# Expert blocks and query weights loaded in pairs, with one more block ahead of the parked ones

## The chip, the cores and the metric

The kernel runs on one core of a Trainium2 chip. The metric is the device time of one execution in microseconds (us). Three runs of the kernel before took 2314.72, 2319.04 and 2312.84 us, median 2314.72. Engines are called PE (matmul), DVE (vector), ACT (scalar), POOL (GpSimd) and SP (sync, which here only issues DMAs).

## What is computed

Two transformer blocks over 512 tokens of width 1024, in fp32. The first block ends in a product-key expert layer, and this is where the change lies. Cut to what matters:

```python
def peer(xn, w_query, sub_keys, u_tab, v_tab):          # per chunk of 128 tokens
    q = (xc @ w_query).reshape(c, PEER_HEADS, 2, D_HALF)
    sc = jnp.einsum('chpd,hpkd->chpk', q, sub_keys)      # 8 heads, 2 halves, 128 keys
    sv, si = lax.top_k(sc, PEER_TOPK)                    # 16 of 128, twice
    ...                                                  # 16 of the 256 pairs: idx, g
    a = gelu(jnp.einsum('chkd,cd->chk', u_tab[idx], xc))
    return jnp.einsum('chk,chkd->cd', g * a, v_tab[idx]) # u_tab, v_tab: 16384 x 1024
```

Every token uses 8 x 16 = 128 of the 16384 experts. The second block (`dilated_mixture_attention`, `spatial_gating` and a gated feed-forward) is not touched.

## The kernel before, in words

All large products are done as three matmuls on fp32r parts (`mm3`, lines 135 to 138): a weight block is loaded raw, ACT copies it to the part `whi` and DVE subtracts to get `wlo`. `wload` (lines 125 to 133) does so for one block of 128x1024 fp32, 4096 bytes per partition, from a pool with three raw buffers and, in the expert stage, four buffers each of `whi` and `wlo` (pool `wpb`, line 399).

The expert layer is done in two ways. Token tile 0 gathers its 2 x 128 expert rows per token by indirect DMA from POOL (`gather_steps`, lines 458 to 477). Tiles 1 to 3 (384 tokens) meet all 16384 experts in 128 dense blocks of 128 experts: the first product (`hps`, 24 matmuls of 384 columns), Gelu, a multiplication with the gate matrix, and the second product into six accumulators (`acc`, 18 matmuls of 512 columns). Three stages follow each other:

1. Routing (about 380 to 880 us). Sixteen blocks of query weights (line 509), the top-16 searches on DVE, then `gate_matrix`, which writes the dense gate matrix to DRAM as `wdr`. Between these steps `park_blocks` computes the first product of 68 expert blocks (`NPARK`, blocks `NLEAD` to `NLEAD` + 67) and stores it in DRAM as `park`. The instruction order of this stage is the planner's, which works from its own costs.
2. The lead (about 880 to 908 us), lines 706 to 717: the `NLEAD` = 3 blocks in front of the parked ones are split and multiplied.
3. The dense loop (908 to 1699 us), lines 719 to 734: iteration n loads what block n+3 needs (`dload`), splits v of block n+2 and u of block n+2 where it is not parked (`dsplit`), does `h_stage(n+1)` and then the second product `v_stage(n)`. For a parked block `h_stage` only reloads `hg` from `park`. Every eighth iteration begins with `wtile`, which reads the next eight blocks' slab of the gate matrix, 1536 KB in runs of 512 bytes, into one of two `wt` buffers; the slab before last must have been used up by `hw` (line 685).

Lead and loop stand in `tc.manual_schedule()`: there each engine issues its instructions in the order in which the code emits them, and an instruction that waits holds up all behind it on its engine. In the loop v blocks use the pool `wd`, with three raw and three split buffers of 4096 bytes per partition.

Of the kernel before, what the change touches and what calls it, by code (L numbers as in the profile page):

```python
# [8 lines left out]
F32 = mybir.dt.float32  # L9
F32R = mybir.dt.float32r  # L10
# [3 lines left out]
AF = mybir.ActivationFunctionType  # L14
# [8 lines left out]
NEG = -1e30  # L23
NPARK = 68                                # blocks of expert activations computed during the routing
NLEAD = 3                                 # blocks in front of the parked ones
PARKS = ((), (2, 1), (2, 2), (2, 1))      # parked blocks per group of a tile's gate matrix, even and odd
GATH = (0, 1, 3, 3)                       # gathers per group of a tile's gate matrix
RATE = (0.9, 2.5)                         # gathers per dense block, parked and not
DECODE = {(1, 1): 0, (1, 4): 2, (2, 3): 3}
# [12 lines left out]
def body(ctx: ExitStack, tc: tile.TileContext, A: dict, out: bass.AP):  # L42
# [13 lines left out]
    def sqrt_ahead(after):  # L56
        """Has the activation table of Sqrt loaded before the chain that needs it."""
        w = sm.tile([128, 1], F32, name="warm", bufs=1)
        SC.activation(w, after, AF.Square)
        SC.activation(w, w, AF.Sqrt)  # L60
# [13 lines left out]
    def rstd_newton(var, which):  # L74
        """1 / sqrt(var + eps) by three Newton steps from the exponent-halving guess, on the vector engine alone."""
        w = sm.tile([128, 4], F32, name="nw")
        x, y, a, r = [w[:, k:k + 1] for k in range(4)]
        V.tensor_scalar(x, var, (1e-5, 1e-6)[which], None, op0=OP.add)
        V.tensor_scalar(a.bitcast(U32), x.bitcast(U32), 1, None, op0=OP.logical_shift_right)
        V.tensor_scalar(y.bitcast(U32), a.bitcast(U32), -1.0, 1597463007.0, op0=OP.mult, op1=OP.add)  # L80
        for c in (-3.0, -12.0, -768.0):
            V.scalar_tensor_tensor(a, x, y, y, op0=OP.mult, op1=OP.mult)
            V.scalar_tensor_tensor(y, a, c, y, op0=OP.add, op1=OP.mult)
        V.tensor_scalar(r, y, -1.0 / 8192.0, None, op0=OP.mult)
        return r
# [14 lines left out]
    def first_half(junk_pool, y):  # L100
        """mean square of a row's first half, halved, plus the norm's eps"""
        ss = sumsq(junk_pool, y, 512)
        b = sm.tile([128, 1], F32, name="half")
        V.tensor_scalar(b, ss, 1.0 / D, 1e-6, op0=OP.mult, op1=OP.add)
        return b
# [48 lines left out]

    def halves(mm_pool, srcs, xh, xl, fill, parts=(0, 1)):
        """The blocks of srcs, two token tiles ahead of the other two; fill() readies those."""
        ws = [wload(src, [128, ND, 128]) for src in srcs]
        pss = [mm_pool.tile([128, S], F32, name="mm", tag="mm") for _ in srcs]
        for part in parts:
            sl = slice(part * 256, part * 256 + 256)  # L160
            if part == parts[1]:
                fill()
            for (wh, wl), ps in zip(ws, pss):
                fm_block(ps[:, sl], wh, wl, xh[:, :, sl], xl[:, :, sl], ND)
        return pss
# [25 lines left out]

    # ------------------------------------------------ first block: mixers
    with ExitStack() as st:
# [14 lines left out]
        with ExitStack() as s1:  # L208
            wk = s1.enter_context(tc.tile_pool(name="wkn", bufs=2, reuse_waits="tile"))
            xts = []  # L210
            for t in range(NT):
                xt = wk.tile([128, D], F32, name="xt", bufs=4)
                SY.dma_start(xt, A["x"][t * 128:(t + 1) * 128, :])
                xts.append(xt)
                if t == 0:
                    g_mix = gain("g_mix")
                    SY.dma_start(ident, A["ident"])

            def xs_of(t):
                xt = xts[t]  # L220
                r = rstd_of(sumsq(wk, xt, D), D, 0)
                xs = wk.tile([128, D], F32, name="xs")
                V.scalar_tensor_tensor(xs, xt, r, g_mix, op0=OP.mult, op1=OP.mult)
                return xs

            to_feature(pst, xs_of, xh, xl, (0, 1))
            first[8], first[9] = halves(pmm, [A["w_in"][8], A["w_in"][9]], xh, xl,
                                        lambda: to_feature(pst, xs_of, xh, xl, (2, 3)))
# [166 lines left out]

    # ------------------------------------------------ product-key experts
    # token tile 0 gathers its expert rows; the other tiles meet every expert on the tensor engine
    with ExitStack() as st:
        wp = st.enter_context(tc.tile_pool(name="wpb", bufs=4, reuse_waits="tile"))
        wps.append(wp)  # L400
# [24 lines left out]
        with ExitStack() as s1:  # L425
            wk = s1.enter_context(tc.tile_pool(name="wk2", bufs=2, reuse_waits="tile"))
            pst = s1.enter_context(tc.tile_pool(name="pst2", bufs=2, space=PSUM, side="right", reuse_waits="tile"))

            def xs_of(t):
                xt = hres[:, t, :]  # L430
                r = rstd_of(sumsq(wk, xt, D), D, 0)
                xs = xtok if t == 0 else wk.tile([128, D], F32, name="xs")
                V.scalar_tensor_tensor(xs, xt, r, gff, op0=OP.mult, op1=OP.mult)
                return xs

            with tc.high_priority():
                to_feature(pst, xs_of, xh, xl, (0, 1))

            def rest():
                with tc.high_priority():  # L440
                    to_feature(pst, xs_of, xh, xl, (2, 3))

            first = halves(pmm, [A["w_query"][0], A["w_query"][1]], xh, xl, rest)

        def h_block(n):
            uh, ul = wload(A["u_cols"][n], [128, ND, 128])
            ps = psh.tile([128, TD], F32, name="hps", tag="hps")
# [5 lines left out]
        def park_blocks():  # L453
            for n in range(NPARK):
                SY.dma_start(park[n], h_block(NLEAD + n))
                yield

# [28 lines left out]
        with mix as s1:  # L486
# [18 lines left out]
            for hp_ in range(16):  # L505
                if hp_ < len(first):
                    ps = first[hp_]
                else:
                    wh, wl = wload(A["w_query"][hp_], [128, ND, 128])
                    ps = pmm.tile([128, S], F32, name="mm", tag="mm")  # L510
# [14 lines left out]
                if hp_ % 2 == 0:  # L525
                    continue
                # a pair (a, b) has (a + 1)(b + 1) - 1 pairs before it in the order, so b < 4 once a >= 4
                h = hp_ // 2
# [111 lines left out]
        def dload(kind, n):  # L640
            if n >= 128:
                return
            if kind == "u":
                if parked(n):
# [3 lines left out]
                    return  # L648
                pool, src = wp, A["u_cols"][n].rearrange("p k j -> p (k j)")
            else:  # L650
                pool, src = wd, A["v_experts"][n * 128:(n + 1) * 128, :]
            raw = pool.tile([128, D], F32, name="wraw", tag="wraw", bufs=3)
            SY.dma_start(raw, src)
            raws[kind, n] = raw

# [49 lines left out]
        with tc.manual_schedule():  # L705
# [3 lines left out]
            for m in range(3):  # L709
                dload("v", m)  # L710
            dload("u", NLEAD)
            for m in range(NLEAD):
                dsplit("u", m)
            for m in range(2):
                dsplit("v", m)
            for m in range(NLEAD):
                h_stage(m)
            done = 0
            for n in range(128):
                if n % 8 == 0:  # L720
                    wtile(n // 8 + 1)
                dload("v", n + 3)
                if n + 3 > NLEAD:
                    dload("u", n + 3)
                if n + 2 >= NLEAD:
                    dsplit("u", n + 2)
                dsplit("v", n + 2)
                want = int(min(n + 1, 71) * RATE[0] + max(n - 70, 0) * RATE[1])
                spread(gathers, (want - done) // 2)
# [17 lines left out]

    # ------------------------------------------------ second block
    with ExitStack() as st:
# [9 lines left out]
        with ExitStack() as s2:  # L759
# [193 lines left out]
            def to_y(c, t, ps):  # L953
# [3 lines left out]
                else:  # L957
# [7 lines left out]
                    if t > 1:  # L965
# [3 lines left out]

            pss = halves(pmm, [A[w][c] for c in range(2) for w in ("w_gate", "w_up")], x4h, x4l,  # L970
                         lambda: to_feature(pst, lambda t: yt[:, t, :], x4h, x4l, (1, 0)), (1, 0))
# [55 lines left out]


def _part(v):
    return np.ascontiguousarray(v.reshape(-1, 128).T)  # L1030


def prepare(I):
# [17 lines left out]
    A["w_o"] = _rows(I["w_o"][0])  # L1051
    A["w_query"] = _cols(I["w_query"][0])
    A["sub_keys"] = I["sub_keys"][0].reshape(16, 128, 128).transpose(0, 2, 1)
    A["u_experts"] = I["u_experts"][0]
    A["u_cols"] = I["u_experts"][0].reshape(128, 128, ND, 128).transpose(0, 3, 2, 1)
    A["v_experts"] = I["v_experts"][0]
    A["ln_final_g"] = I["ln_final_g"]
    A["positions"] = _part(I["positions_2"][0])
# [38 lines left out]
```

## Time and profile before

| | us |
|---|---|
| median of three runs | 2314.72 |
| lowest and highest | 2312.84, 2319.04 |
| span of the profiled execution | 2313.5 |
| expert stage within it | about 380 to 1699 |

The profiled execution's span is 1.2 us below the median of the runs; nothing else of it lies outside the span in what is shown. The page lists for each engine its busy time, in 40 slices of the span how busy it was, which clock PE was granted, and how busy the 16 DMA engines were. For a change in one stage the questions are which engine is busy without a gap there, and what the gaps wait for.

### The profile page before, as it was taken

To read this page: it belongs to the slowest core of one execution; us is meant where nothing else is said; L and a number is where in the kernel's file an instruction comes from. 1 tells how busy PE (TensorE), PEld (TensorE's weight loads), DVE (VectorE), ACT (ScalarE), POOL (GpSimd) and SP (SyncE) were. 2 spreads that over 40 slices of the span, in tenths; PEclk is the share of its full clock that TensorE was granted. 3 is DMA by queue.
4 is the path that set the end of the run, shared out by engine and by line. 5 is a ranking of instruction groups with operands and counts; after the bars stand their busy time and mean duration, and the time that the engine had idled before them with its cause. 6 is when DMAs were issued, how large, how long until landed. Compare 5 with 4: busy or idle time off the path is not lost.

```text
span 2313.5 us, 30184 instructions
## 1 busy us (share of the span) xinstructions
PE 2246.8 (97%) x11337; PEld 1931.4 (83%) x11337; DVE 1495.2 (65%) x2998; ACT 986.1 (43%) x1631; POOL 382.4 (17%) x261
## 2 busy tenths in 40 slices
PE   7999998999899999999999999999999999999998
PEld 6768887989799999777779999999976778888886
DVE  4553254989999994767777777777784555333323
ACT  4354233333897783333333333333353364322222
POOL 0000000000222430323323444444400000000000
PEclk9999999999899999999999999999999999999999
DMA  5202232443577997889899898889732112333331
GB/s 173 92 19 75 90 111 84 128 125 118 213 272 289 363 350 253 295 311 329 293 323 322 306 320 297 296 302 323 274 113 74 56 55 87 105 101 93 98 100 65
DMA packets 177572, 444.82 MB, mean 192 GB/s; under 512 B 15249, under 2 KB 84241, under 8 KB 174353
## 3 DMA queue, kind: packets, MB, share of 16 engines
q1 hardware_dynamic: 140560, 308.65, 39.8%
q0 software_dynamic: 36864, 134.23, 16.3%
q8 instruction: 89, 1.46, 0.2%
q14 instruction: 59, 0.48, 0.1%
HBM read 402.19 MB, written 40.63 MB: 191 GB/s over the span
## 4 chain that ended last, share of the span: by engine, by line
PE 86%; DVE 5%; ACT 4%; DMA 4%; issue 1%; DVEq 0%; ACTq 0%; SPq 0%
PE mm L136 13%; PE mm L137 12%; PE mm L138 12%; PE hps L138 7%; PE hps L136 7%; PE hps L137 7%; PE acc L136 6%; PE acc L138 6%; PE acc L137 6%; DMA wraw<-in_v_experts_dram 3%; PE wps L612 2%; PE sc L311 1%; PE pv L346 1%; ACT stg L614 1%; PE sc L889 1%
## 5 line engine op out<-in xcount | busy, mean ns | idle before, releaser
L130 ACT ACTIVATE whi<-wraw 128x1024 fp32r<-128x1024 f32 x232 | 241.8, 1045 | 568.9 <-PE mm L137 343.0
L132 DVE TENSOR_TENSOR wlo<-wraw,whi 128x1024 fp32r<-128x1024 f32 x232 | 278.7, 1204 | 265.9 <-ACT whi L130 261.5
L136 PE MATMUL hps<-x2h,whi 128*128 128x384 f32 x1024 | 348.1, 340 | 2.1 <-ACT whi L130 1.8
L138 PE MATMUL hps<-x2h,wlo 128*128 128x384 f32 x1024 | 345.1, 337 | 0.8 <-DVE wlo L132 0.8
L137 PE MATMUL hps<-x2l,whi 128*128 128x384 f32 x1024 | 344.2, 336 | 0.0
L464 POOL DMA_INDIRECT gu<-in_u_experts_dram,ix x128 | 190.8, 1491 | 914.0 <-PE wps L612 605.5
L136 PE MATMUL acc<-whi,hh 128*128 128x512 f32 x768 | 302.6, 394 | 17.3 <-ACT hh L117 17.3
L138 PE MATMUL acc<-whi,hl 128*128 128x512 f32 x768 | 303.2, 395 | 0.0
L137 PE MATMUL acc<-wlo,hh 128*128 128x512 f32 x768 | 302.7, 394 | 0.0
L664 DVE TENSOR_TENSOR wlo<-wraw,whi 128x1024 fp32r<-128x1024 f32 x188 | 227.5, 1223 | 74.6 <-ACT whi L662 69.0
L662 ACT ACTIVATE whi<-wraw 128x1024 fp32r<-128x1024 f32 x188 | 198.3, 1056 | 171.3 <-issue 85.5
L473 POOL DMA_INDIRECT gv<-in_v_experts_dram,ix x128 | 189.7, 1482 | 380.7 <-DVE hres L475 275.3
L136 PEld LDWEIGHTS hps<-x2h,whi 128*128 128x128 f32 x1024 | 193.3, 189 | 5.4 <-ACT whi L130 2.1
L137 PEld LDWEIGHTS hps<-x2l,whi 128*128 128x128 f32 x1024 | 193.1, 189 | 2.7
L138 PEld LDWEIGHTS hps<-x2h,wlo 128*128 128x128 f32 x1024 | 193.1, 189 | 1.1 <-DVE wlo L132 1.1
L136 PEld LDWEIGHTS acc<-whi,hh 128*128 128x128 f32 x768 | 145.5, 189 | 49.6 <-ACT hh L117 21.0
L138 PEld LDWEIGHTS acc<-whi,hl 128*128 128x128 f32 x768 | 145.8, 190 | 33.3 <-DVE hl L118 2.7
L137 PEld LDWEIGHTS acc<-wlo,hh 128*128 128x128 f32 x768 | 145.7, 190 | 29.3
L475 DVE SCALAR_TENSOR_TENSOR hres<-gv,ga,hres 128x1024 f32<-128x1024 f32 x128 | 164.1, 1282 | 1.0
L466 DVE CUSTOM_DVE_ANT_0 gu<-gu,xtok 128x1024 f32<-128x1024 f32 x128 | 154.5, 1222 | 0.0
L137 PE MATMUL mm<-x4l,whi 128*128 128x512 f32 (+1 forms) x384 | 143.9, 375 | 0.0
L136 PE MATMUL mm<-x4h,whi 128*128 128x512 f32 (+1 forms) x384 | 143.3, 376 | 0.3 <-ACT x4h L117 0.3
(316 smaller groups left out, 4022.3 us busy)
## 6 DMA issues: line engine op xcount, KB each, us to landing
wraw<-in_u_cols_dram SPq DMA_DIRECT2D x128, 512.0 KB
wraw<-in_v_experts_dram SPq DMA_DIRECT2D x128, 512.0 KB
wraw<-in_w_in_dram SPq DMA_DIRECT2D x50, 512.0 KB
wdr<-stg SPq DMA_DIRECT2D x24, 1024.0 KB
wt<-wdr SPq DMA_DIRECT2D x16, 1536.0 KB
park<-hg SPq DMA_DIRECT2D x68, 192.0 KB
hg<-park SPq DMA_DIRECT2D x68, 192.0 KB
wraw<-in_w_gate_dram SPq DMA_DIRECT2D x22, 512.0 KB
```

Source lines behind the costliest of these rows:

```text
L130: SC.activation(hi, raw, AF.Copy)
L132: V.tensor_tensor(lo, raw, f(hi), op=OP.subtract)
L136: PE.matmul(ps, lhsT=ah, rhs=bh, start=start, stop=False)
L137: PE.matmul(ps, lhsT=ah, rhs=bl, start=False, stop=False)
L138: PE.matmul(ps, lhsT=al, rhs=bh, start=False, stop=stop)
L464: GP.indirect_dma_start(out=u, out_offset=None, in_=A["u_experts"], in_offset=bass.IndirectOffsetOnAxis(ap=ix[:, s_:s_ + 1], axis=0))
L466: V.tensor_tensor_reduce(out=u, in0=u, in1=xtok, scale=1.0, scalar=0.0, op0=OP.mult, op1=OP.add, accum_out=a[:, s_:s_ + 1])
L473: GP.indirect_dma_start(out=v, out_offset=None, in_=A["v_experts"], in_offset=bass.IndirectOffsetOnAxis(ap=ix[:, s_:s_ + 1], axis=0))
L475: V.scalar_tensor_tensor(hres[:, 0, :], v, a[:, s_:s_ + 1], hres[:, 0, :], op0=OP.mult, op1=OP.add)
L612: PE.matmul(ps[:, k, :], lhsT=oj[:, 4 * e + k, :], rhs=og)
L662: SC.activation(hi, raw, AF.Copy)
L664: V.tensor_tensor(lo, raw, f(hi), op=OP.subtract)
```

## The change

u, v and the query weights are laid out in DRAM by pairs of blocks, so that one DMA brings two blocks, 8192 bytes in one run per partition, 1024 KB in all. Raw buffers: two pairs (tag `wraw2`) in place of three single blocks, in `wpb` (u and query weights) and in `wd` (v). The split buffers of `wpb` go from four to three. `NLEAD` goes from 3 to 4, so that pairs stay whole; 68 blocks stay parked. In the lead each block's u split, its v split (for the first two) and its `h_stage` now follow one another, where before all splits came first. The loop loads pair (n+4, n+5) in every even iteration. Comments are gone.

```diff
-NLEAD = 3
+NLEAD = 4
...
+    def pair(src):
+        raw = wps[-1].tile([128, 2, D], F32, name="wraw", tag="wraw2", bufs=2)
+        SY.dma_start(raw, src)
+        return raw
+
+    def parts_of(raw, r):
+        hi = wps[-1].tile([128, D], F32R, name="whi", tag="whi")
+        SC.activation(hi, raw[:, r, :], AF.Copy)
+        lo = wps[-1].tile([128, D], F32R, name="wlo", tag="wlo")
+        V.tensor_tensor(lo, raw[:, r, :], f(hi), op=OP.subtract)
+        return [y.rearrange("p (k j) -> p k j", k=ND) for y in (hi, lo)]
...
-        wp = st.enter_context(tc.tile_pool(name="wpb", bufs=4, reuse_waits="tile"))
+        wp = st.enter_context(tc.tile_pool(name="wpb", bufs=3, reuse_waits="tile"))
...
-            first = halves(pmm, [A["w_query"][0], A["w_query"][1]], xh, xl, rest)
+            raw = pair(A["w_query"][0])
+            first = halves(pmm, [parts_of(raw, 0), parts_of(raw, 1)], xh, xl, rest)
...
-            for n in range(NPARK):
-                SY.dma_start(park[n], h_block(NLEAD + n))
-                yield
+            for n in range(0, NPARK, 2):
+                raw = pair(A["u_cols"][(NLEAD + n) // 2])
+                for r in range(2):
+                    SY.dma_start(park[n + r], h_block(*parts_of(raw, r)))
+                    yield
...
-                    wh, wl = wload(A["w_query"][hp_], [128, ND, 128])
+                    if hp_ % 2 == 0:
+                        raw = pair(A["w_query"][hp_ // 2])
+                    wh, wl = parts_of(raw, hp_ % 2)
...
-            raw = pool.tile([128, D], F32, name="wraw", tag="wraw", bufs=3)
-            SY.dma_start(raw, src)
-            raws[kind, n] = raw
+            if n % 2 == 0:
+                raw = pool.tile([128, 2, D], F32, name="wraw", tag="wraw2", bufs=2)
+                SY.dma_start(raw, src[n // 2])
+                raws[kind, n] = raw[:, 0, :]
+                raws[kind, n + 1] = raw[:, 1, :]
...
-            dload("u", NLEAD)
             for m in range(NLEAD):
                 dsplit("u", m)
-            for m in range(2):
-                dsplit("v", m)
-            for m in range(NLEAD):
+                if m < 2:
+                    dsplit("v", m)
                 h_stage(m)
             done = 0
             for n in range(128):
                 if n % 8 == 0:
                     wtile(n // 8 + 1)
-                dload("v", n + 3)
-                if n + 3 > NLEAD:
-                    dload("u", n + 3)
+                dload("v", n + 4)
+                dload("u", n + 4)
...
-                want = int(min(n + 1, 71) * RATE[0] + max(n - 70, 0) * RATE[1])
+                want = int(min(n + 1, 72) * RATE[0] + max(n - 71, 0) * RATE[1])
...
+def _pairs(w):
+    return np.ascontiguousarray(w.reshape(w.shape[0] // 2, 2, 128, -1).transpose(0, 2, 1, 3))
...
-    A["w_query"] = _cols(I["w_query"][0])
+    A["w_query"] = _pairs(_cols(I["w_query"][0]))
...
-    A["u_cols"] = I["u_experts"][0].reshape(128, 128, ND, 128).transpose(0, 3, 2, 1)
+    A["u_cols"] = _pairs(I["u_experts"][0].reshape(128, 128, ND, 128).transpose(0, 3, 2, 1))
...
+    A["v_rows"] = _pairs(I["v_experts"][0].reshape(128, 128, D))
```

## Rows read from the trace of the kernel before

**Rows 1.** The page: busy us, share of the span, instructions; then PE's clock.
```profile
PE 2246.8 (97%) x11337; PEld 1931.4 (83%) x11337; DVE 1495.2 (65%) x2998; ACT 986.1 (43%) x1631; POOL 382.4 (17%) x261
...
PEclk9999999999899999999999999999999999999999
```

**Rows 2.** Windows (us): length, busy us and instructions per engine, PEclk, DMA share, GB/s.
```profile
575.00:700.00 125.00, 111.73 (x690) 106.47 (x689) 116.90 (x217) 112.12 (x227) 28.74 (x19) 0.95 0.67 243
700.00:900.00 200.00, 199.00 (x1304) 197.06 (x1303) 177.56 (x321) 143.12 (x249) 56.08 (x40) 1.00 0.89 324
1210.00:1500.00 290.00, 290.00 (x1463) 263.40 (x1463) 223.87 (x270) 106.99 (x143) 123.74 (x85) 1.00 0.89 308
```

**Rows 3.** Waits, 895 to 1215 us: who for whom, total us, times, longest.
```profile
ACT whi L662 <- DMA wraw<-in_v_experts_dram: 30.8, 12, 4.9
...
PEld acc L136 <- ACT hh L117: 21.0, 9, 4.0
```

**Rows 4.** SP's timeline in the parked stretch: start us, us, what is issued.
```profile
927.37 0.33 SPq L653 DMA_DIRECT2D wraw<-in_v_experts_dram  x1
...
931.45 0.33 SPq L653 DMA_DIRECT2D wraw<-in_v_experts_dram  x1
...
935.99 0.38 SPq L670 DMA_DIRECT2D wt<-wdr  x1
936.48 5.18 SPq L653 DMA_DIRECT2D wraw<-in_v_experts_dram  x1
...
1189.49 0.37 SPq L670 DMA_DIRECT2D wt<-wdr  x1
```

**Rows 5.** ACT's timeline around the first and last table; in brackets idle before, releaser.
```profile
941.34 1.06 ACT L662 ACTIVATE whi<-wraw 128x1024 fp32r<-128x1024 f32 x1 [0.73 <-PE acc L138]
...
949.21 1.06 ACT L662 ACTIVATE whi<-wraw 128x1024 fp32r<-128x1024 f32 x1 [4.52 <-DMA wraw<-in_v_experts_dram]
952.02 0.52 ACT L117 ACTIVATE hh<-hw 128x384 fp32r<-128x384 f32 x1 [1.76 <-DVE hw L685]
...
1201.28 1.06 ACT L662 ACTIVATE whi<-wraw 128x1024 fp32r<-128x1024 f32 x1 [2.99 <-DMA wraw<-in_v_experts_dram]
```

**Rows 6.** PE's weight loads behind that first table.
```profile
952.60 0.19 PEld L136 LDWEIGHTS acc<-whi,hh 128*128 128x128 f32 x1 [3.61 <-ACT hh L117]
```

**Rows 7.** Windows behind the stalls of the first and third table.
```profile
953.00:957.00 4.00, 4.00 (x13) 3.08 (x12) 3.41 (x5) 1.51 (x2) 1.68 (x1) 0.65 0.74 249
...
1026.00:1030.00 4.00, 2.46 (x10) 1.87 (x11) 3.41 (x6) 1.47 (x2) 0.51 (x1) 1.00 1.03 401
```

**Rows 8.** DMA in 931 to 937 us: packets, MB, rate, packets by size.
```profile
DMA packets 650, 1.75 MB, mean 292 GB/s; under 512 B 83, under 2 KB 306, under 8 KB 650
```

**Rows 9.** DMA in 945 to 949.2 us, behind a table; then SP's queue alone.
```profile
DMA packets 548, 1.69 MB, mean 402 GB/s; under 512 B 54, under 2 KB 190, under 8 KB 547
...
q1 hardware_dynamic: 414, 1.19, 72.5%
```

**Rows 10.** DMA in 1085 to 1089 us, nearly all of it a table.
```profile
DMA packets 2361, 1.22 MB, mean 305 GB/s; under 512 B 3, under 2 KB 2358, under 8 KB 2361
```

**Rows 11.** ACT's timeline, last parked blocks and lead.
```profile
879.32 1.06 ACT L130 ACTIVATE whi<-wraw 128x1024 fp32r<-128x1024 f32 x1 [2.90 <-PE hps L137]
...
894.10 1.06 ACT L662 ACTIVATE whi<-wraw 128x1024 fp32r<-128x1024 f32 x1 [0.87 <-DMA wraw<-in_v_experts_dram]
...
900.34 0.49 ACT L681 ACTIVATE hg<-hps 128x384 f32<-128x384 f32 x1 [3.13 <-issue]
...
908.66 0.49 ACT L681 ACTIVATE hg<-hps 128x384 f32<-128x384 f32 x1 [2.52 <-PE hps L138]
...
910.21 1.04 ACT L662 ACTIVATE whi<-wraw 128x1024 fp32r<-128x1024 f32 x1
```

**Rows 12.** DVE's timeline behind that last Gelu of the lead.
```profile
911.28 1.23 DVE L664 TENSOR_TENSOR wlo<-wraw,whi 128x1024 fp32r<-128x1024 f32 x1 [0.39 <-ACT whi L662]
```

**Rows 13.** The chain that ended last, start of the expert stage: start us, us, what.
```profile
380.46 5.58 DMA wraw<-in_w_query_dram
```

More of the change, by code (lines that the diff above doesn't have):

```diff
@@ L153, in fm_block, with halves @@
             mm3(ps, wh[:, k, :], wl[:, k, :], xh[:, k, :], xl[:, k, :], k == 0, k == nk - 1)
-    def halves(mm_pool, srcs, xh, xl, fill, parts=(0, 1)):
-        ws = [wload(src, [128, ND, 128]) for src in srcs]
-        pss = [mm_pool.tile([128, S], F32, name="mm", tag="mm") for _ in srcs]
+    def pair(src):
[8 more added lines that the diff above has]
+        return [y.rearrange("p (k j) -> p k j", k=ND) for y in (hi, lo)]
+    def halves(mm_pool, ws, xh, xl, fill, parts=(0, 1)):
+        pss = [mm_pool.tile([128, S], F32, name="mm", tag="mm") for _ in ws]
         for part in parts:
@@ L226, in body @@
             to_feature(pst, xs_of, xh, xl, (0, 1))
-            first[8], first[9] = halves(pmm, [A["w_in"][8], A["w_in"][9]], xh, xl,
+            first[8], first[9] = halves(pmm, [wload(A["w_in"][c], [128, ND, 128]) for c in (8, 9)], xh, xl,
                                         lambda: to_feature(pst, xs_of, xh, xl, (2, 3)))
@@ L441, in rest, with h_block @@
                     to_feature(pst, xs_of, xh, xl, (2, 3))
-            first = halves(pmm, [A["w_query"][0], A["w_query"][1]], xh, xl, rest)
-        def h_block(n):
-            uh, ul = wload(A["u_cols"][n], [128, ND, 128])
+            raw = pair(A["w_query"][0])
+            first = halves(pmm, [parts_of(raw, 0), parts_of(raw, 1)], xh, xl, rest)
+        def h_block(uh, ul):
             ps = psh.tile([128, TD], F32, name="hps", tag="hps")
@@ L648, in dload @@
                     return
-                pool, src = wp, A["u_cols"][n].rearrange("p k j -> p (k j)")
+                pool, src = wp, A["u_cols"]
             else:
-                pool, src = wd, A["v_experts"][n * 128:(n + 1) * 128, :]
-            raw = pool.tile([128, D], F32, name="wraw", tag="wraw", bufs=3)
-            SY.dma_start(raw, src)
-            raws[kind, n] = raw
+                pool, src = wd, A["v_rows"]
+            if n % 2 == 0:
[3 more added lines that the diff above has]
+                raws[kind, n + 1] = raw[:, 1, :]
         def dsplit(kind, n):
@@ L968, in body @@
             token_major([pmm] * 4, "w_out_2", range(2), ND, lambda k, sl: ch[k // 4][:, k % 4, sl], lambda k, sl: cl[k // 4][:, k % 4, sl], to_y, group=3, order=(3, 2, 1, 0))
-            pss = halves(pmm, [A[w][c] for c in range(2) for w in ("w_gate", "w_up")], x4h, x4l,
+            pss = halves(pmm, [wload(A[w][c], [128, ND, 128]) for c in range(2) for w in ("w_gate", "w_up")], x4h, x4l,
                          lambda: to_feature(pst, lambda t: yt[:, t, :], x4h, x4l, (1, 0)), (1, 0))
```

## The prediction

> **What bounds the kernel now.** I read the page first, then windows by stage, then waits, and last the timelines of single engines where a gap stood. PE is busy for 97% of the span and at full clock in nearly all of it [rows 1], so any change pays only where PE has gaps. The windows show where: from 1210 us on, where each block also has its first product, PE is busy for 290 of 290 us, and in 700 to 900 us for 199 of 200 [rows 2]. There faster loads can give nothing. Two stretches have gaps: 575 to 700 us in the routing (111.73 of 125 us busy [rows 2], gaps behind ACT and DVE work), and the parked part of the dense loop, about 905 to 1210 us.
>
> The parked part is the one that the change aims at, so it is read closely. SP issues a v load every 4.08 us when nothing disturbs [rows 4]; this is one block of 18 matmuls. Every eighth block SP first issues the table (`wt`, line 670), 1.57 MB in runs of 512 bytes, and the v load of block 8g+3 comes right behind it, its issue itself held for 5.18 us [rows 4]. That load is late: ACT waits 4.52 us for it at the first table and 2.99 us at the last [rows 5]. Behind the waiting split stands `hh` on ACT, and behind `hh` PE, which is idle for 3.61 us [rows 5, 6]. In all ACT waits 30.8 us for v loads [rows 3]; 27.8 us of it are the eight tables (n = 8 to 64). An undisturbed split waits 0.73 us for PE anyway [rows 5], so a table makes its block late by 27.8/8 - 0.73 = 2.75 us. What it costs in time: from the first to the eighth table 253.5 us pass [rows 4] for 56 blocks, 56 x 4.08 = 228.5 us, hence 25 us for seven stalls, with about 2.2 for the eighth **27 us**. That is 22 us of lateness and 5 us in which PE ran slowly afterwards: behind the 3.61 us gap the granted clock is 0.65 of full and 13 matmuls go in 4 us, where 17.6 would; behind a shorter one it stays at 1.00 [rows 7]. This 27 us is all the dense part can give back.
>
> **Part 1, the order behind a table: a gain.** The table's issue does not move: it waits for `hw` of block 8g-1, before and after. But v of 8g+3 now comes in one pair with 8g+2, ahead of the table, and the pair behind the table starts with 8g+4, which is wanted one block, 4.08 us, later. Against that stand two losses. The pair has landed only when its second half has, 0.52 MB more; SP's queue moves 1.19 MB in 4.2 us behind a table, 285 GB/s [rows 9], so 1.8 us. And 0.52 MB more stand ahead of the table; around its issue the DMA engines move 292 GB/s on average [rows 8], so at most 1.8 us, at least 0 if they had been idle; I take 0.9. The new lateness is 2.75 - 4.08 + 1.8 + 0.9 = 1.4 us a table, 11 us for eight; with 1 us of slow clock, since the gaps are now short, 12 us. The **gain is 27 - 12 = 15 us** (bounds: 27 if both losses vanish, 5 if the pair lands as late as sketched under the rivals). Pairs elsewhere have time: a pair is issued when the split of the block three before it is through, as a single load was, and has about 10 us (three blocks less 2.3 us for that split) for 1.05 MB, 3.7 us at 285 GB/s, plus at most 3.7 us that are not transfer (5.58 us for a load of 0.52 MB at the start [rows 13], less 1.8).
>
> I count the 8192-byte run itself as nothing: loads in runs of 4096 bytes already bring the DMA engines to 402 GB/s [rows 9], and it is the table, at 305 GB/s almost alone [rows 10], that is slow, and it stays as it is. Here a rule of the Trainium skill speaks for more ("DMA: Bandwidth & Descriptors", sections "Rules for kernel authors" and "Anatomy of one DMA"): at least 1 MiB per DMA for full rate, since each carries about 2 us that do not scale. By that fit a pair would land 2 us sooner than two single loads one after the other, and the gain would be the whole 27 us. The row speaks against it: loads queued on one ring overlap, so the fixed part is already hidden.
>
> **Part 2, the lead: a loss.** This is the step easily overlooked. Before, all splits stood ahead of the first `h_stage`, and PE ran the three lead blocks without a gap, 4.16 us each (Gelus at 900.34 and 908.66, two blocks apart [rows 11]). With three split buffers u of block 3 can't be split before block 0 is done, and the code now interleaves: on ACT the split of u(m+1) stands behind Gelu and `hh` of block m, and the code's order is kept. So PE can't start block m+1 while ACT waits for the end of block m. The rows give the delay exactly, since the same chain stands behind the last lead block: Gelu at 908.66, `hw`, `hh`, the next split on ACT from 910.21 [rows 11], its `wlo` from 911.28 for 1.23 us [rows 12], thus 3.85 us after the Gelu began. The third matmul of a block needs `wlo`; unhindered it starts with that Gelu, give or take 0.1 us, since PE ends one block and begins the next without a gap. That is 3.8 us for each of three transitions, **11.4 us**, and nothing covers it: all parked blocks come earlier on PE and `v_stage(0)` later. Each gap is about 2.7 us and then another 1 us. Gaps of 3.6 us cost 1.2 to 1.6 us in slow clock, 2.4 us ones none [rows 7]; I take 1.2 each, 3.6 (0 to 4.8). Further, the second u pair can only be loaded once the last parked block is split, one block later than at 879.32 for want of the fourth buffer; table 0 and v(0) queue behind it, with 1.05 MB more ahead of them or with them. From 894.10 [rows 11] v(0) moves by 4.2 + 1.05 MB/402 GB/s = 6.8 us to 900.9, and its split now stands ahead of the first Gelu at 900.34: 1 us (0 to 2). **Sum 16 us** (11.4 to 18.2). The fourth lead block itself is free, since the tail has one less.
>
> **Part 3, the routing: about nothing, with an unknown order.** The first query pair is on the chain: 5.58 us from issue to landing [rows 13]. It now must land whole; 0.52 MB at 402 GB/s is 1.3 us, part of which moved in that time already: 1 us (0.5 to 1.3). With one split buffer fewer the split of a block waits for PE's end of the block three before it rather than four; already now the splits are released by PE [rows 11], and PE still has two blocks, 8.3 us, in hand against 2.3 us of splitting. So it costs nothing as long as pairs land in time; what falls due next if not is PE itself. Between 700 and 900 us PE has 1 us to lose back [rows 2] and only losses are possible, between 575 and 700 us 13 us of gaps may shrink or grow. The planner makes a new order from other load sizes, which no row can show; I take +1 (-6 to +8).
>
> **Part 4, no change.** The later dense part: PE is full (1463 matmuls in 290 us [rows 2], 42 a block, thus 8.3 us a block), and a pair of u or v has three blocks, 25 us. Splits, matmuls, gathers and bytes stay the same in number. Gathers end one iteration later, in DVE time that is idle then; if not, 1 us.
>
> Sum: -15 + 16 + 1 + 1 = +3 on the profiled 2313.5, which is 1.2 below the median: **2318 us**.
>
> **Rivals.** *The table's stall goes entirely* (the page's rule, or the queue passes the table sooner than I think): -27 + 16 + 2 = -9; with a lead whose clock doesn't fall (11.4) and a routing 4 us better, -18: 2297 to 2306. For it speaks that the slack of one block (4.08) is above the mean lateness (2.75); against, that bytes behind the table double. *The pair lands nearly as late as the single load did*: the pair ahead pushes the table by 1.4 us, and SP's queue falls to 225 GB/s beside the gathers, 2.3 us for the second half: lateness 2.75 - 4.08 + 1.4 + 2.3 = 2.4, gain 3 to 5 us, with a full lead loss of 18 and 2 in the routing +15 to +17: about 2331. It decides once the new lateness at a table is above 1.9 us; from there the lead's loss is more than 7 us above the gain. *The change does not do what it says*: if the 8192-byte runs go as two packets each, nothing changes, since my sum gives them no worth. *The planner's new order* keeps PE waiting in the routing: the 13 us of gaps doubled would give 2331 as well.
>
> **How the numbers follow.** A measurement of this kernel can tell about 0.3%, 7 us, from no change. My forecast (gain and loss cancel, 2308 to 2321, likeliest value 2318) gets 0.44; the rival without stall 0.20; lateness staying 0.24 and a worse routing 0.12, both on the slower side, where my sum already leans. So faster 0.20, same 0.44, slower 0.36. The range takes in most of both rivals: 2301 to 2334.
>
> **What would show it.** ACT's waits for v loads in the parked stretch fall from 30.8 us to about half; the wait sits at blocks 8g+4, not 8g+3, and distances between tables fall from 36 to about 34.5 us. In the lead the Gelus (line 681's counterpart) stand near 8 us apart, three times, where they stood 4.16 apart. If they stand 4.16 apart, part 2 is wrong and the kernel is some 15 us faster; if tables still stand 36 us apart, part 1 is wrong and it is slower. PE's busy share in 575 to 900 us tells part 3.

## The result and the profile after

Four runs of the changed kernel take 2337.79 us in the median (2335.23 to 2350.56), beside 2315.99 for the kernel before in the same comparison: ratio 1.0105 with the interval 1.0077 to 1.0134. It is 1% slower, and 3.8 us above the range that was given. The profiled execution has a span of 2336.8 us, 23.3 above the one before.

First the page, for [rows 1]: PE is busy 8 us longer for the same 11337 matmuls, and the DMA line says how many packets lie under a size.

```profile
PE 2255.1 (97%) x11337; PEld 1938.4 (83%) x11337; DVE 1496.2 (64%) x2998; ACT 983.5 (42%) x1630; POOL 374.9 (16%) x261
...
PEclk9999999999899999999999999999999999999999
...
DMA packets 157985, 444.78 MB, mean 190 GB/s; under 512 B 13073, under 2 KB 82065, under 8 KB 137361
```

20,624 packets are now of 8 KB or more (before, 3,219), so the long runs do exist; the rival by which the change doesn't do what it says is out.

The windows of the changed kernel, for [rows 2]: length, busy us and instructions per engine, clock, DMA share, GB/s. The second row was 199.00 of 200.

```profile
575.00:700.00 125.00, 110.20 (x685) 104.14 (x684) 116.66 (x215) 110.47 (x224) 27.66 (x19) 0.95 0.68 245
...
700.00:900.00 200.00, 195.79 (x1272) 194.30 (x1271) 174.52 (x318) 140.38 (x246) 53.16 (x40) 0.98 0.86 313
```

PE does 4.7 us less work up to 900 us, and the Gelu of the last parked block starts 5.3 us later (902.01, before 896.73): the routing has lost.

Then the lead, ACT's timeline, for [rows 11]: start us, us, instruction, in brackets idle time before it and its releaser.

```profile
906.57 1.06 ACT L680 ACTIVATE whi<-wraw 128x1024 fp32r<-128x1024 f32 x1 [4.06 <-DMA wraw<-in_v_rows_dram]
907.53 0.47 ACT L699 ACTIVATE hg<-hps 128x384 f32<-128x384 f32 x1
909.82 1.99 ACT L680 ACTIVATE whi<-wraw 128x1024 fp32r<-128x1024 f32 x2
918.45 0.49 ACT L699 ACTIVATE hg<-hps 128x384 f32<-128x384 f32 x1 [6.65 <-issue]
920.00 1.04 ACT L680 ACTIVATE whi<-wraw 128x1024 fp32r<-128x1024 f32 x1
926.53 0.49 ACT L699 ACTIVATE hg<-hps 128x384 f32<-128x384 f32 x1 [5.49 <-issue]
928.07 1.04 ACT L680 ACTIVATE whi<-wraw 128x1024 fp32r<-128x1024 f32 x1
936.19 0.49 ACT L699 ACTIVATE hg<-hps 128x384 f32<-128x384 f32 x1 [7.08 <-issue]
```

The Gelus of the four lead blocks stand 10.9, 8.1 and 9.7 us apart, where they stood 4.16 apart. Each split of the next block stands behind the Gelu of the block before, and PE waits for it. The window of the lead shows PE with the same columns:

```profile
907.00:937.00 30.00, 19.11 (x77) 17.14 (x78) 9.58 (x12) 7.83 (x12) 0.00 (x0) 0.83 0.37 113
```

It idles 10.9 of 30 us, and 77 matmuls take 19.1 us at a mean clock of 0.83 of the full 2.4 GHz, where 24 of them took 4.16 us before, so 77 would take 13.3.

Last the dense loop. SP's timeline at the first table and at the last one, for [rows 4], and ACT's splits behind these two, for [rows 5]:

```profile
958.99 0.33 SPq L670 DMA_DIRECT2D wraw<-in_v_rows_dram  x1
959.45 4.39 SPq L662 DMA_DIRECT2D hg<-park  x2
963.90 0.44 SPq L688 DMA_DIRECT2D wt<-wdr  x1
967.15 3.94 SPq L670 DMA_DIRECT2D wraw<-in_v_rows_dram  x1
...
1216.31 0.43 SPq L688 DMA_DIRECT2D wt<-wdr  x1
```

```profile
979.80 1.06 ACT L680 ACTIVATE whi<-wraw 128x1024 fp32r<-128x1024 f32 x1 [3.49 <-DMA wraw<-in_v_rows_dram]
...
1232.63 1.06 ACT L680 ACTIVATE whi<-wraw 128x1024 fp32r<-128x1024 f32 x1 [3.85 <-DMA wraw<-in_v_rows_dram]
```

From the first to the eighth table 252.4 us pass, before 253.5 [rows 4]: of the 15 us that were to come back here, 1 has. The waits between 910 and 1240 us, for [rows 3] (who for whom, total us, times, longest), show the same, and the new wait of the lead:

```profile
ACT whi L680 <- DMA wraw<-in_v_rows_dram: 27.6, 8, 4.3
...
PEld acc L136 <- ACT hh L117: 20.4, 8, 3.4
...
PE hps L136 <- ACT whi L680: 10.3, 3, 4.8
```

The wait has moved from block 8g+3 to block 8g+4 as predicted, eight times, and is as long as it was.

So the 23.3 us add up: routing 5.3; the lead 22.2 up to the first product into `acc` (which starts at 935.94, before 908.41, 27.5 later in all), of which 4.2 is the fourth lead block; the loop from that product to the last one 787.3 in place of 790.5, although it has 4.2 less to do, thus +1; and 1 less behind it.

### The profile page after: what moved, and what is told of

It is laid out like the page before. It is cut to its first block, busy times and chain, and to the rows that moved or that the text cites. A ratio compares the mean times of both kernels' runs of the same rounds, so it can differ in the third digit from the quotient of the medians.

```text
span 2336.8 us, 29893 instructions
## 1 busy us (share of the span) xinstructions
PE 2255.1 (97%) x11337; PEld 1938.4 (83%) x11337; DVE 1496.2 (64%) x2998; ACT 983.5 (42%) x1630; POOL 374.9 (16%) x261
## 4 chain that ended last, share of the span: by engine, by line
PE 52%; DMA 4%; DVE 2%; ACT 1%; issue 0%; DVEq 0%; ACTq 0%
PE mm L136 7%; PE mm L137 7%; PE mm L138 7%; PE acc L136 6%; PE acc L138 6%; PE acc L137 6%; DMA wraw<-in_v_rows_dram 4%; PE hps L138 3%; PE hps L136 3%; PE hps L137 3%; PE sc L904 1%; PE pv L930 1%; DVE wlo L682 1%; ACT whi L680 1%; PE tr L923 0%; PE tr L148 0%
## 5 line engine op out<-in xcount | busy, mean ns | idle before, releaser
L132 DVE TENSOR_TENSOR wlo<-wraw,whi 128x1024 fp32r<-128x1024 f32 (+1 forms) x148 | 176.7, 1195 | 243.3 <-ACT whi L130 240.4
L130 ACT ACTIVATE whi<-wraw 128x1024 fp32r<-128x1024 f32 (+1 forms) x148 | 153.3, 1036 | 424.8 <-PE mm L137 281.3
L682 DVE TENSOR_TENSOR wlo<-wraw,whi 128x1024 fp32r<-128x1024 f32 x188 | 227.3, 1222 | 81.7 <-ACT whi L680 79.1
L680 ACT ACTIVATE whi<-wraw 128x1024 fp32r<-128x1024 f32 x188 | 198.0, 1055 | 171.7 <-PE acc L138 94.6
L487 POOL DMA_INDIRECT gv<-in_v_experts_dram,ix x128 | 183.5, 1433 | 410.2 <-DVE hres L489 316.2
L163 ACT ACTIVATE whi<-wraw 128x1024 fp32r<-128x1024 f32 x84 | 88.5, 1058 | 146.9 <-PE hps L137 82.2
```

What stands on the lines that cost most here:

```text
L130: SC.activation(hi, raw, AF.Copy)
L132: V.tensor_tensor(lo, raw, f(hi), op=OP.subtract)
L163: SC.activation(hi, raw[:, r, :], AF.Copy)
L487: GP.indirect_dma_start(out=v, out_offset=None, in_=A["v_experts"], in_offset=bass.IndirectOffsetOnAxis(ap=ix[:, s_:s_ + 1], axis=0))
L680: SC.activation(hi, raw, AF.Copy)
L682: V.tensor_tensor(lo, raw, f(hi), op=OP.subtract)
```

## The experiments

Medians of each run stand beside those of the kernel before on the same chip, 2314.30 us for the first four experiments and 2314.81 for the last four. "Above before" is the difference to these; the changed kernel itself is 21.8 above before (2337.79 against 2315.99). Views of the trace are of one profiled execution of each kernel.

**The lead's order alone.** The changed kernel, its lead in an order that needs three split buffers and yet lets PE run on: the splits of three blocks first, that of the fourth behind the first `h_stage`.

```diff
-            for m in range(NLEAD):
+            for m in range(3):
                 dsplit("u", m)
-                if m < 2:
-                    dsplit("v", m)
+            for m in range(2):
+                dsplit("v", m)
+            h_stage(0)
+            dsplit("u", 3)
+            for m in range(1, NLEAD):
                 h_stage(m)
```

> The changed kernel with the lead's order alone put right: u of blocks 0 to 2 and v of 0 and 1 split first, then the first product of block 0, the split of u of block 3, and the products of blocks 1 to 3. Buffers, pairs and loop as in the changed kernel. Theory (the interleaved order makes PE wait for each next split): the Gelus of the lead stand about 4.2 us apart instead of 8 to 11, the first second product starts near 919 us instead of 935.9, and the kernel gains 15 to 18 us, to about 2321. Rival (PE is held by table 0 and the first v pair, which land only at 906 us, and the order merely shows it): the first second product moves by less than 8 us and so does the time.

Measured: 2322.32 us (2317.03 to 2324.13), 8.0 above before, ratio 1.0031 (1.0019 to 1.0042), so 13.8 of the 21.8 us are gone. ACT's timeline of this kernel, the four Gelus of the lead:

```profile
904.78 0.47 ACT L699 ACTIVATE hg<-hps 128x384 f32<-128x384 f32 x1
...
908.20 0.47 ACT L699 ACTIVATE hg<-hps 128x384 f32<-128x384 f32 x1
910.75 0.49 ACT L699 ACTIVATE hg<-hps 128x384 f32<-128x384 f32 x1 [0.17 <-PE hps L138]
914.90 0.49 ACT L699 ACTIVATE hg<-hps 128x384 f32<-128x384 f32 x1 [2.52 <-PE hps L138]
```

They are 10.1 us from first to last, in the changed kernel it was 28.7. The first product into `acc` starts at 914.66, 21.3 earlier than in the changed kernel; 3.0 of this come from the routing, which this edit does not touch (last parked Gelu at 899.0 in place of 902.0). Some of it is lost again, since the first and the eighth table are now 257.8 us apart and not 252.4; why is open. The emission order of the lead is thus shown to cost about 14 to 16 us (13.8 by the medians, 16.2 by the spans of the profiled executions).

**Two DMAs for a pair of v.** The changed kernel, each v pair loaded as two DMAs of 512 KB, one for each block, so that the first block needn't wait for the second.

```diff
-                SY.dma_start(raw, src[n // 2])
+                if kind == "v":
+                    for r in range(2):
+                        SY.dma_start(raw[:, r, :], src[n // 2][:, r, :])
+                else:
+                    SY.dma_start(raw, src[n // 2])
```

> The changed kernel with each v pair loaded by two DMAs of 512 KB, one per block, into the same pair buffer in the same places of the queue (runs of 4096 bytes). Theory A (behind a table the first block waits for the second half of its pair): ACT's waits at the eight tables fall from 3.4 us on average by about 1.8, and the kernel gains 14 to 18 us, to 2320 to 2324. Theory B (what counts is the bytes queued ahead of the pair, table and pair before it): waits and time change by less than 4 us.

Measured: 2326.43 us (2318.79 to 2328.90), 12.1 above before, ratio 1.0042 (1.0026 to 1.0057). ACT's waits of this kernel, 910 to 1240 us:

```profile
ACT whi L684 <- DMA wraw<-in_v_rows_dram: 15.9, 6, 3.7
...
PEld acc L136 <- ACT hh L117: 12.9, 7, 2.8
```

The wait for v falls from 27.6 to 15.9 us and seven table distances from 252.4 to 242.9, a loss of 14.4 against 228.5 undisturbed (23.9 in the changed kernel). So 40% of the stall is the second half of the pair; the other 60% remain with the pair's first half behind the table as well. The 9.7 us by which the kernel gains on the changed one are less than the 14 to 18 of theory A, and more than the 4 of theory B: neither accounts for it alone.

**Short runs in one DMA.** The changed kernel, each v pair still one DMA of 1024 KB, but read from the unpaired layout in runs of 4096 bytes.

```diff
-                SY.dma_start(raw, src[n // 2])
+                if kind == "v":
+                    SY.dma_start(raw, A["v_experts"][n * 128:(n + 2) * 128, :].rearrange("(r p) d -> p r d", r=2))
+                else:
+                    SY.dma_start(raw, src[n // 2])
```

> The changed kernel with each v pair loaded by one DMA of 1024 KB as before, but from the unpaired layout, so in runs of 4096 bytes instead of 8192. Theory (the run's length is worth nothing): landing of the pair behind a table stays at 15.7 us after the table's issue within 0.5, the time within 4 us. Rival (long runs carry data faster): landings 1 us or more later, the kernel 8 us or more slower. Second rival (long runs are themselves what makes pairs land late): 1 us or more earlier, 8 us or more faster.

Measured: 2337.35 us (2335.25 to 2340.64), 23.0 above before, ratio 1.0108 (1.0091 to 1.0125); the changed kernel has 1.0105. Seven table distances take 250.2 us, the first table's split waits 4.01 us. The length of the run is worth nothing here; what acts is that two blocks come in one DMA, as the run above shows.

**The table one block later.** The changed kernel with the table issued in odd iterations, behind which no pair is loaded at once.

```diff
-                if n % 8 == 0:
+                if n % 8 == 1:
```

> The changed kernel with the table issued one iteration later (n % 8 == 1), so just behind the issue of a v pair instead of just ahead of one. Theory (the pair behind the table misses a deadline set by the place of the table between two pair issues: from the table's issue to the turn of the pair's first block there are now 13.1 us and landing takes 15.7; one iteration later there would be 17.5): the waits at tables nearly vanish and the kernel gains 20 to 27 us, to about 2312 to 2318. Rival (the queue is simply short of time around a table, wherever it stands): the wait moves to the next pair and the time changes by less than 5 us.

Measured: 2327.23 us (2323.38 to 2328.78), 12.9 above before, ratio 1.0062 (1.0045 to 1.0079). ACT's waits of this kernel, 910 to 1240 us:

```profile
ACT whi L680 <- DMA wraw<-in_v_rows_dram: 14.1, 6, 3.4
...
PE acc L136 <- ACT hh L117: 6.4, 5, 2.0
```

Seven distances take 238.0 us: a loss of 9.5, in place of 23.9. A block more of time for the table takes away over half of the stall and not all of it: the pair that it delays is then the one of 8g+6, and this still comes late at six of eight tables. There the split starts 17.6 to 19.6 us after the table's issue, where the eight of the changed kernel started after 15.8 in the mean: the expectation gave the pair 4 us more and took its landing as unchanged, but at these six it came about 2.8 us later. By the medians less than half of the expected gain came, 8.9 us; the profiled execution, the fastest of the four, is 15.2 us shorter than that of the changed kernel.

**Both of them.** The lead's order and the table in odd iterations together.

> The changed kernel with both single edits that gained: the lead's splits ahead of its products (15.5 us alone) and the table behind a pair's issue instead of ahead of one (10.6 us alone). Theory (two separate losses, one in the lead, one in the parked stretch): they add up, 26 us less than the changed kernel, about 2312. Rival (the lead's stalls had given the queue time that the tables then lack): together less than 20, above 2318.

Measured: 2307.98 us (2303.51 to 2315.95), 6.8 below before, ratio 0.9970 (0.9956 to 0.9985). Alone the two parts lie 13.8 and 8.9 us below the changed kernel, together 28.6, more than their sum of 22.7. The profiled executions are 16.2, 15.2 and 29.7 us shorter than that of the changed kernel, which is a little less than the sum; so the two losses add up about as the theory says, and the rival is out. Here too the lead's order costs something at the tables: seven distances take 242.2 us, without it 238.0. With two edits of order the change is a small gain.

**Only the fourth split buffer.** The kernel before, with nothing changed but the number of split buffers of u and the query weights.

```diff
-        wp = st.enter_context(tc.tile_pool(name="wpb", bufs=4, reuse_waits="tile"))
+        wp = st.enter_context(tc.tile_pool(name="wpb", bufs=3, reuse_waits="tile"))
```

> The kernel before with three split buffers of u and query weights instead of four, nothing else. Theory (the fourth buffer is what the routing stage loses by: splits come one block later, and the planner orders around it): the last parked Gelu moves from 896.7 to 900 us or later, the kernel is 3 to 8 us slower. Rival (the routing loses by the pair loads, not by the buffer): within 2.5 us of before.

Measured: 2325.91 us (2322.04 to 2326.58), 11.1 above before, ratio 1.0043 (1.0029 to 1.0058). Its windows, with the columns of [rows 2]:

```profile
575.00:700.00 125.00, 109.42 (x681) 103.42 (x680) 116.27 (x220) 109.27 (x223) 27.21 (x19) 0.95 0.68 238
...
700.00:900.00 200.00, 194.16 (x1270) 192.68 (x1269) 176.47 (x320) 141.92 (x249) 53.06 (x40) 0.99 0.88 314
```

Single loads and three split buffers lose 7.1 us of PE's work before 900 us, pairs and three split buffers 4.7. The first product into `acc` starts at 916.50, 8.1 later than before; the loop behind it takes 793.3 us in place of 790.5. The last parked Gelu stands at 905.0; in the kernels with pairs, whose routing code is the same, it stands between 899.0 and 904.1, and in the two profiled with four buffers at 896.7 and 894.6. So the buffer alone makes at least the routing's loss, and no loss by the pairs is seen beside it, within the 5 us by which equal routings differ. The kernel loses more than the 3 to 8 us that were expected. Which planned step needs the fourth buffer the runs do not tell, and why the loop takes 2.8 us longer stays open as well. Four buffers beside the pairs were not tried.

**The table in four parts.** The kernel before, each table read by four DMAs of 384 KB, one in each of the first four iterations of eight.

```diff
-                SY.dma_start(wt, wdr[:, :, 8 * g:8 * g + 8, :].rearrange("g j i t -> j g i t"))
                 wts[g] = wt
+        def wpart(g, k):
+            if g < 16:
+                gs = slice(6 * k, 6 * k + 6)
+                SY.dma_start(wts[g][:, gs], wdr[gs, :, 8 * g:8 * g + 8, :].rearrange("g j i t -> j g i t"))
...
             wtile(0)
+            for k in range(4):
+                wpart(0, k)
...
                     wtile(n // 8 + 1)
+                if n % 8 < 4:
+                    wpart(n // 8 + 1, n % 8)
                 dload("v", n + 3)
```

> The kernel before with each table read in four DMAs of 384 KB (six of its 24 groups each), one in each of the iterations 8g to 8g+3, instead of one of 1536 KB; same bytes, same runs of 512 bytes, same buffers. Theory (a table stalls PE because one v load stands behind all of it): ACT's waits for v loads nearly vanish, tables stand 33 us apart, and the kernel gains 20 to 27 us, to about 2290. Rival (the parked stretch is short of DMA time as such, 0.90 of it being busy): the waits spread over four blocks and the gain is below 8 us.

Measured: 2286.52 us (2285.16 to 2286.90), 28.3 below before, ratio 0.9874 (0.9857 to 0.9890), the fastest of all. The window from 910 to 1210 us, first of the kernel before, then of this one:

```profile
910.00:1210.00 300.00, 282.71 (x1203) 228.74 (x1202) 218.31 (x292) 105.83 (x136) 95.28 (x59) 0.98 0.89 304
```

```profile
910.00:1210.00 300.00, 299.80 (x1329) 247.95 (x1328) 239.22 (x315) 117.06 (x149) 109.24 (x64) 1.00 0.96 336
```

And who waits in this kernel, 910 to 1240 us:

```profile
ACT whi L662 <- DMA wraw<-in_v_experts_dram: 4.9, 4, 1.4
...
PE acc L136 <- ACT hh L117: 0.2, 1, 0.2
```

PE has 17 us of gaps in the one and 0.2 in the other, and the bytes to be loaded are the same. The parked loop's loss was therefore not the bytes but that 1536 KB stood in one piece ahead of a load that was due. Smaller DMAs and their spread over four iterations were not tried apart.

**The same on the changed kernel,** with the lead's order of the first experiment.

> The changed kernel with the lead put right and each table read in four DMAs in four iterations, as in the other run on the kernel before. Theory (pairs cost nothing once neither lead nor tables stall; what stays is the routing's 5 us and the start): about 5 us behind the kernel before with the same parts. Rival (pairs need the room that parts leave, their 1 MB being a burst of its own): 10 us or more behind it.

Measured: 2294.02 us (2290.03 to 2295.53), 20.8 below before, ratio 0.9904 (0.9888 to 0.9921), but 7.5 above the kernel before with its table in parts. No wait for v is left in its parked stretch. From the first to the last product into `acc` it takes 758.7 us, the other kernel 764.4 with one block more, 4.2 us; the loops are level to 1.5 us. The first product starts at 918.80 against 906.60, 12.2 later, of which the fourth lead block is 4.2. The other 8 are the routing's: its last parked Gelu stands at 903.15, in the other kernel at 894.58. The 7.5 us lie between the 5 of the theory and the 10 of the rival; with the wait for v gone they come from ahead of the loop, as the theory has it, and the pairs give back no more than the loop's 1.5.

## Why the prediction was wrong

**What bounds the kernel: right.** The 27 us for the tables were read right: with the table in parts 28.3 us come back, 26.1 of them between the first and the last product into `acc` (764.4 us in place of 790.5), and PE is busy for 299.80 of 300 us.

**Part 1: the step that failed.** The lateness of the pair behind a table was to be 2.75 - 4.08 + 1.8 + 0.9 = 1.4 us. The term of 0.9 for what stands ahead of the table was mis-sized, at half of what it measures, and its reason was wrong. ACT's wait gives the time from the table's issue to the landing at each table: before 13.1, 13.5, 11.9, 10.7, 12.0, 11.9, 11.8 and 11.7 us (mean 12.1), after 15.8, 16.6, 13.9, 14.7, 16.4, 16.2, 16.0 and 16.2 (mean 15.7). That is 3.6 us more and not 2.7. The DMA view of the stretch from one table's issue to the landing (packets, MB, share of 16 engines) shows more bytes in it; first the kernel before, 1081.06 to 1093.1 us, then the changed one, 1104.27 to 1120.7:

```profile
q1 hardware_dynamic: 3460, 2.57, 70.0%
```

```profile
q1 hardware_dynamic: 3816, 3.84, 70.0%
```

At this table SP's queue carries 1.27 MB more, over all eight 1.00 MB in the mean (0.43 to 1.40): at 285 GB/s these would be 3.5 us. I had counted the pair's second half, 0.52 MB, in full, and half of the 0.52 MB that the pair ahead of the table has more than a single load. But the pair ahead is not what the table waits for. The changed kernel's issues of 1099.38 to 1104.27 us, with the time from issue to landing (of two, the median) at the end of each line:

```profile
wt<-wdr SPq DMA_DIRECT2D x1, 1536.0 KB, 12.6
wraw<-in_v_rows_dram SPq DMA_DIRECT2D x1, 1024.0 KB, 4.9
hg<-park SPq DMA_DIRECT2D x2, 192.0 KB, 6.6
```

The pair issued at 1099.38 lands after 4.9 us, just as the table is issued; at all eight tables it lands within 0.4 us of that. The table itself is late: it lands 12.6 us after its issue, 12.1 in the mean of eight, which is as long as the table and the load behind it took together before (12.1). From there to the landing of the pair it is another 3.6 us in the mean, 1.05 MB at 285 GB/s. So, as an estimate, the second half costs the 1.8 us that I gave it, and the table comes another 1.8 later. The queues in the two us behind the table's issue, again the kernel before first, 1081.06 to 1083.06 us, then the changed one, 1104.27 to 1106.27 (q0 are the gathers, q1 is SP's queue; packets, MB, share):

```profile
q0 software_dynamic: 54, 0.19, 42.0%
q1 hardware_dynamic: 36, 0.03, 4.4%
```

```profile
q0 software_dynamic: 109, 0.38, 66.8%
q1 hardware_dynamic: 110, 0.14, 20.9%
```

Gathers move more there, 0.38 MB in place of 0.19 (in the mean of eight tables 0.30 in place of 0.17), and SP's queue still has the two loads of parked activations to bring, which land 6.6 us after their issues. Before, one such load was issued 4.07 us ahead of the table. Now they are loaded four blocks ahead with four `hg` buffers, as many as before, so that the second of the two waits for the same `hw` as the table and is issued 0.37 us ahead of it. The prediction has no term for either. How much of the 1.8 us each of them makes, no run shows: this cause stays open.

With 1.8 in place of 0.9, and the table issued 0.37 us nearer to the pair's turn (at the first table 13.14 us lie between them, where 9.43 + 4.08 were to be expected), the lateness is 2.75 - 4.08 + 3.64 + 0.37 = 2.7 us: as late as before. This is the second rival, with its condition (more than 1.9 us) met; its own sum of 2.4 was near, but by luck in one term, since the pair ahead, which was to push the table by 1.4 us, had landed. The smallest gain of 5 us was no bound either: it was that rival's upper value, and the 0.37 us a table, 3 us for eight, was in neither.

The runs agree that there are two parts: the second half alone is 40% of the stall (two DMAs for a pair), and what remains goes when the table does (in parts). One more difference was not tried alone: with two raw pairs the pair behind the table is issued 3.25 us after it (963.90 and 967.15), where the single load came 0.49 us after it. At all eight tables the issue is then held for another 2.44 to 4.63 us, so I read that wait as covered.

**The rule of 1 MiB.** For full bandwidth a DMA should carry at least 1 MiB (the Trainium skill, "DMA: Bandwidth & Descriptors", "Rules for kernel authors"). The first rival had all 27 us come back by it; 1 did. Two DMAs of 512 KB in place of one of 1024 KB are 9.7 us faster here: the pair's first block is due first, and in one DMA it has to wait for the second.

**Run length: right.** It was counted as nothing, and with runs of half the length the time is 2337.35 us.

**Part 2, the lead: right.** 16 us were predicted (11.4 for three transitions, 3.6 for the clock, 1 for v(0)). Measured from Gelu to Gelu the three transitions take 28.7 us in place of 12.5, 16.2 more, and the first Gelu comes 7.2 later, 5.3 of it from the routing and 1.9 from v(0): 18.1, at the upper bound of 18.2. The sizes within the sum were off: the slow clock cost 5.8 us (19.1 against 13.3 for 77 matmuls), above its bound of 4.8, which leaves 10.4 of the 16.2 for the gaps in place of 11.4, and v(0) landed at 906.5 us, not at 900.9. The first experiment takes this part away and gains 14 to 16 us.

**Part 3, the routing: failed.** "So it costs nothing as long as pairs land in time" is the step. With one split buffer fewer and nothing else the kernel before loses 11.1 us, 8.1 of them ahead of the loop. I had argued from the end of the routing, where PE has two blocks in hand and splits wait for PE; that doesn't hold for 575 to 900 us, where PE loses 7.1 us of work in that run and 4.7 in the changed kernel. A range of -6 to +8 held the 5.3 us of the changed kernel, and the value in it was 1 + 1. The rival of the planner's order (gaps doubled, +13 us) was the right place, though its size was more than twice too large and the cause is the buffer count and not the size of the loads.

**Part 4: right to 2 us.** The loop beside its tables takes 2 us more (1 more in all, 1 less at the tables), the tail 1 less.

The sum as it came out: -1 + 18 + 5 + 2 - 1 = 23 in place of -15 + 16 + 1 + 1 = 3. Of the 20 us between them 14 are Part 1, 2 are Part 2, 3 are Part 3 and 1 is Part 4.

## What to carry to other kernels

Where a bulk transfer shares a queue with loads that are due every few microseconds, count everything that moves between its issue and its landing: its own second half, what is still queued ahead of the bulk, and other queues on the same DMA engines. Cut the bulk and spread it rather than making the small ones larger: the same table in four parts over four iterations is worth 28 us here, and loads of double size are worth nothing. A buffer that is given up to make room has to be costed by itself, over the whole stage in which it is used. And where the code's order is an engine's order, look at what a moved line now stands behind: two edits of order alone turn this change from 22 us slower to 7 us faster.

## What was not expected of the hardware

The issue of a load on SP takes 0.33 us, but behind the eight tables 3.80 to 5.61 us before and 2.44 to 4.63 in the changed kernel, and the next issue stands behind it.

A longer queue raised the rate little. SP's queue moves 2.57 MB in 12.0 us at a table before, 214 GB/s, and 3.84 MB in 16.4 us after, 234 GB/s, beside the gathers; over the eight tables it is 215 and 229. With runs of 8192 bytes the eight splits behind a table wait 3.45 us in the mean, with runs of 4096 bytes 3.44.
